# Heads in pairs on TensorE: scores from the two halves of the rows, values into the two halves of a bank

## The chip, the cores and the metric

The kernel runs on one core of one Trainium2 chip, as one program of 24,835 profiled instructions. The metric is the device time of one execution in microseconds, median of several runs. Engines are named as in the profile: PE is TensorE, PEld its weight loads, DVE is VectorE, ACT is ScalarE, POOL is GpSimd, SP is SyncE.

## What is computed

Two transformer blocks over 256 tokens of width 1024, in float32. The first has a gated spatial mixer, six heads of forgetting attention (fox: scores with a decay) and four heads that attend to 256 memory tokens, then a feed-forward layer. The second has two layers; each is a gated feed-forward layer, an attention, and another feed-forward layer. Its first attention is a sliding window with 16 heads over two key and value heads, its second a latent attention with 16 heads, whose queries and keys are 64 + 32 wide.

```python
# forgetting attention                       # memory attention
s = q @ k.T * scale + c_t - c_s              s = q @ km.T * scale
p = softmax(where(causal, s, NEG))           p = softmax(s)
o = p @ v                                    o = p @ vm
# sliding window                             # latent attention
scores = q @ k.T * scale + bias              s = q @ k.T * scale      # q, k 96 wide
p = softmax over window, with a sink         p = softmax(where(causal, s, NEG))
o = p @ v                                    o = p @ v
x = x + o.reshape(tokens, heads * 64) @ w_out
```

A head is 64 wide in the first three kinds.

## The kernel before

Nearly all the time goes into products of weights and activations. Weights come from HBM in chunks; `Stream` (`ws`) splits each into a high part (ScalarE, L102) and a low part (VectorE, L112), and every product is made of three passes in a reduced float32 format: high by high, high by low, low by high (`mm_t` L139 to L141, `mm_n` L149 to L151). The program is in order on each engine as it is written; the tile framework puts in the waits. PSUM has eight banks, handed out one tile a bank by `bank()`.

The attention of the heads is in plain float32, and one matmul of it stands in the trace as two records. It is made by `Pipe`, a pipeline by hand over heads ("units"), whose `step` is called between pieces of the weight products, so that TensorE has other work while VectorE and ScalarE do the softmax. Step n does, in this order:

- `score` of unit n (only at the start) and of unit n + 1: `attn_s`, two matmuls of the queries of 128 tokens each against the keys (L297), into a bank of its own. Queries and keys of a head 64 wide lie on rows 0 to 63 (even head) or 64 to 127 (odd head) of their tiles, so that these matmuls use 64 rows of TensorE; those of latent attention use 96. Fox heads then call `pre_fox` (L684, L685), which makes the decay products in another bank.
- `attn_t` of unit n - 2: three or four transpositions of the probabilities on TensorE (L308), and a copy to SBUF by ScalarE (`pt`, L311).
- on VectorE: the front of unit n (bias or mask, maximum: L695 to L705, L712 to L714, L979 to L987, L1215 to L1220), and `attn_tail` of unit n - 1 (reciprocal L286, scaling of the probabilities L289), mixed; then, if one is waiting, the low part of a finished output pair (`ol`, L331).
- `attn_exp` of unit n: exponentials on ScalarE (L271, L275).
- `attn_o` of unit n - 3: values, two matmuls with the 64 columns of the values as weights (L323, and L325 or L327). Even heads write rows 0 to 63 of a bank, odd heads rows 64 to 127 of the same bank; after the odd one ScalarE copies the bank out (`oh`, L330), and the low part is made in the next step (L331).
- `ws.low()`: the low part of the last weight chunk, where one waits (L112).

The pipeline runs three times: in the first block (units 0 to 5 are fox heads, 6 to 9 memory heads; steps among products of the mixer, then the gating matmuls L796), in the sliding window (16 units; two steps for each of the last six query products, with the norm products L995 and VectorE's L997 ahead of the first of them, and the rest in `out_proj_start`), and in latent attention (16 units; transpositions of the heads' keys and queries, L1228 and L1230, between the steps). Memory heads have 256 keys for both token halves (`w=(T, T)`), the others 128 for the first half and 256 for the second (`w=(P, T)`).

Of the kernel before, what the change touches and what calls it, by code (L numbers as in the profile page):

```python
# [9 lines left out]
F32 = mybir.dt.float32  # L10
# [4 lines left out]
ALU = mybir.AluOpType  # L15
AX = mybir.AxisListType

P = 128
T = 256
# [18 lines left out]
R_FORGET, R_SINK, R_QG, R_KG, R_FREQ, N_ROWS = 0, 6, 22, 54, 86, 102  # L38
# [12 lines left out]
def block_kernel(ctx: ExitStack, tc: tile.TileContext, a: dict, out: bass.AP, upto: int = 99):  # L51
# [11 lines left out]
    act, dve, gp, pe = nc.scalar, nc.vector, nc.gpsimd, nc.tensor  # L63

    def bank():
        return psp.tile([P, 512], F32, tag="ps", name="ps")
# [105 lines left out]
    rows = cst.tile([P, N_ROWS], F32, name="rows")  # L172
# [117 lines left out]

        return ops + [scaled(0, slice(0, w0)), scaled(1, slice(w0, w0 + w1))]

    def attn_s(u):
        w0, w1 = u["w"]
        ps = bank()
        for i, (o, n) in enumerate(((0, w0), (w0, w1))):
            pe.matmul(ps[:, o:o + n], lhsT=u["q"][:, i * P:i * P + P], rhs=u["k"][:, :n], start=True, stop=True)  # L297
        u["ps"] = ps
        if "pre" in u:
            u["pre"](u)  # L300

    def attn_t(u):
        w0, w1 = u["w"]
        pr = u["p"]
        pt = bank()
        blocks = [0, P, 2 * P] if w0 == P else [0, 2 * P, P, 3 * P]
        for j, b in enumerate(blocks):
            pe.transpose(pt[:, j * P:j * P + P], pr[:, b:b + P], ident)  # L308
        st = u["pp"].tile([P, w0 + w1], F32, tag="pt", bufs=2, name="pt")
        n = P * len(blocks)  # L310
        act.copy(st[:, :n], pt[:, :n])  # L311
        u["pt"] = st

    opair = {}

    def attn_o(u, oh, ol):
        i = u["o"]
        if i % 2 == 0:
            opair[0] = bank()
        ps = opair[0]  # L320
        r = ps[64 * (i % 2):64 * (i % 2) + 64]
        st, v = u["pt"], u["v"]
        pe.matmul(r[:, 0:T], lhsT=v[0], rhs=st[:, 0:T], start=True, stop=False)  # L323
        if u["w"][0] == P:
            pe.matmul(r[:, P:T], lhsT=v[1], rhs=st[:, T:T + P], start=False, stop=True)  # L325
        else:
            pe.matmul(r[:, 0:T], lhsT=v[1], rhs=st[:, T:2 * T], start=False, stop=True)  # L327
        if i % 2:
            k = i // 2
            act.copy(oh[k], ps[:, :T])  # L330
            opair[1] = lambda: dve.tensor_tensor(out=ol[k], in0=ps[:, :T], in1=oh[k].bitcast(F32), op=ALU.subtract)  # L331

    class Pipe:

# [11 lines left out]
            return self.units[i] if 0 <= i < len(self.units) else None  # L346

        def score(self, i):
            u = self.at(i)
            if u and "ps" not in u:  # L350
                attn_s(u)

        def step(self):
            i = self.n
            new, tail, tr, val = self.at(i), self.at(i - 1), self.at(i - 2), self.at(i - 3)
            self.score(i)
            self.score(i + 1)
            if tr:
                attn_t(tr)
            front = new["front"](new, new["ps"]) if new else []  # L360
            back = attn_tail(tail) if tail else []
            for op in front[:2] + back[:1] + front[2:4] + back[1:2] + front[4:] + back[2:]:
                op()
            if 1 in opair:
                opair.pop(1)()
            if new:
                attn_exp(new)
            if val:
                attn_o(val, self.oh, self.ol)
            ws.low()  # L370
            self.n += 1
            if self.done() and 1 in opair:
                opair.pop(1)()
# [177 lines left out]
    for nm, i0, i1 in seq:  # L551
        for i in range(i0, i1):
            src = [a[nm][i, 0], a[nm][i, 1]] if len(a[nm].shape) == 4 else [a[nm][i]]
            for ap in src:
                n = ap.shape[-1]
# [25 lines left out]
    with ExitStack() as es:  # L581
        mp = es.enter_context(tc.tile_pool(name="mix", bufs=1))
        pp = es.enter_context(tc.tile_pool(name="mixp", bufs=3))
# [8 lines left out]
        oh = [mp.tile([P, T], F32R, name=f"oh{k}") for k in range(KT)]  # L592
        ol = [mp.tile([P, T], F32R, name=f"ol{k}") for k in range(KT)]
# [15 lines left out]
        w = ws.get(0)  # L609
# [7 lines left out]
        for c in range(4):  # L617
            for tt in range(2):
                mm_n(pf[tt][:, :390], w, 0, 390, X, tt, [(2 * c, 0), (2 * c + 1, 1)], c == 0, c == 3)
            w = ws.get(min(4, c + 2))  # L620
# [65 lines left out]

        def front_fox(u, ps):
            h, pb = u["i"], u["pb"]
            s = pp.tile([P, 512], F32, tag="s", bufs=2, name="s")
            mx = sm.tile([P, 2], F32, tag="mx", bufs=3, name="mx")  # L690
            nm = sm.tile([P, 2], F32, tag="nm", bufs=3, name="nm")
            u["s"], u["nm"] = s, nm

            def decayed(i, o, n):
                return lambda: dve.scalar_tensor_tensor(  # L695
                    out=s[:, o:o + n], in0=pb[:, :n], scalar=ct[:, 6 * i + h:6 * i + h + 1],
                    in1=cmask[:, o:o + n], op0=ALU.add, op1=ALU.add)

            def scored(i, o, n):
                return lambda: dve.tensor_tensor_reduce(  # L700
                    out=s[:, o:o + n], in0=ps[:, o:o + n], in1=s[:, o:o + n], scale=1.0,
                    scalar=-3e38, op0=ALU.add, op1=ALU.max, accum_out=mx[:, i:i + 1])

            return [decayed(0, 0, P), decayed(1, P, T), scored(0, 0, P), scored(1, P, T),
                    lambda: dve.tensor_scalar(out=nm, in0=mx, scalar1=-1.0, scalar2=None, op0=ALU.mult)]  # L705
# [15 lines left out]
        for h in range(4):  # L721
            r = slice(64 * (h % 2), 64 * (h % 2) + 64)
            pipe.add(dict(q=mq[h // 2][r], k=km[h // 2][r], v=[vm[0][:, 64 * h:64 * h + 64], vm[1][:, 64 * h:64 * h + 64]],
                          w=(T, T), front=front_mem, o=12 + h))


        for i in range(2):
# [39 lines left out]
        for i in range(3):  # L767
            src = pu[i // 2][:, (i % 2) * T:(i % 2) * T + T]
            tile_x(src)
            if i == 0:  # L770
                vsq = []
                for tt in range(2):
                    act.activation(out=gv[tt], in_=pg[tt][:, :384], func=AF.Gelu_apprx_tanh, scale=rs_x[:, tt:tt + 1])
                    vsq.append(pp.tile([P, 512], F32, tag="s", bufs=2, name="vsq")[:, :384])
                    act.activation(out=vsq[tt], in_=gv[tt], func=AF.Square)
            pipe.step()
            if i == 0:
                for tt in range(2):
                    dve.tensor_reduce(out=vs[:, tt], in_=vsq[tt].rearrange("p (g d) -> p g d", g=6), axis=AX.X, op=ALU.add)
                dve.tensor_scalar(out=vs, in0=vs, scalar1=1.0 / 64, scalar2=EPS, op0=ALU.mult, op1=ALU.add)  # L780
                vr = sm.tile([P, 2, 6], F32, tag="vr", name="vr")
                rstd_pow(vr.rearrange("p a b -> p (a b)"), vs.rearrange("p a b -> p (a b)"), 12)
                for tt in range(2):
                    g3 = gv[tt].rearrange("p (g d) -> p g d", g=6)
                    gp.tensor_tensor(out=g3, in0=g3, in1=vr[:, tt, :, None].to_broadcast([P, 6, 64]), op=ALU.mult)
        for i in range(3):
            src = pu[i // 2][:, (i % 2) * T:(i % 2) * T + T]
            t = pp.tile([P, 512], F32, tag="s", bufs=2, name="ut")[:, :T]
            dve.tensor_tensor(out=t, in0=src, in1=rb, op=ALU.mult)
            act.activation(out=uT[i], in_=t, func=AF.Gelu_apprx_tanh)  # L790
        for j in range(3):
# [108 lines left out]
    with ExitStack() as es:  # L900
# [101 lines left out]
        for i in range(KT):  # L1002
            w = ws.get()
            p = bank()
            mm_t(p[:, :T], w, 0, P, X, range(4), True, False)
            if i == 1:
                pt = bank()
                for h in range(2):
                    for tt in range(2):
                        pe.transpose(pt[:, (2 * h + tt) * P:(2 * h + tt) * P + P], kn[tt][:, h].rearrange("p a d -> p (a d)"), ident)  # L1010
                for h in range(2):
                    act.copy(kT[h], pt[:, h * T:h * T + T])
            if i > 0:
                q_norm(i - 1)
            if i > 1:
                pipe.step()
            mm_t(p[:, :T], w, 0, P, X, range(4, KT), False, True)
            act.activation(out=qT[i], in_=p[:, :T], func=AF.Copy, scale=ga)
            qsq[i] = tp.tile([P, T], F32, tag="sq", name="sq")
            act.activation(out=qsq[i], in_=p[:, :T], func=AF.Square)  # L1020
            for h in (2 * i, 2 * i + 1):
                r = slice(64 * (h % 2), 64 * (h % 2) + 64)
                g = h // 8
                pipe.add(dict(q=qT[i][r], k=kT[g][r], v=[va[0][:, 64 * g:64 * g + 64], va[1][:, 64 * g:64 * g + 64]],
                              w=(P, T), front=front_swa, o=h, sink=rows[:, R_SINK + h:R_SINK + h + 1]))
            if i > 1:
                pipe.step()
        q_norm(KT - 1)
# [432 lines left out]
```

## Time and profile before

| | us |
|---|---|
| median of 3 runs | 1280.71 (1280.48 to 1282.17) |
| profiled execution | 1278.97 |
| its span, first to last instruction | 1277.1 |
| TensorE busy | 1250.2 (98%) |
| VectorE busy | 846.4 (66%) |
| ScalarE busy | 661.3 (52%) |
| mean granted clock of TensorE | 0.989 of full speed |

The busy time of TensorE counts its records from start to modelled end, and these overlap: a matmul's row tells when it starts, and the distance to the next start tells what it costs. "idle before" stands in brackets at the end of a timeline row, with the instruction that ended the wait.

### The profile page before, as it was taken

The page shows a single profiled execution, that of the slowest core. Times are in us where ns is not written, and L with a number is a line of the kernel's source. Part 1 is how long each engine was busy: PE and PEld are TensorE (multiplying, and loading weights), DVE is VectorE, ACT ScalarE, POOL GpSimd, SP SyncE. Part 2 cuts the span into 40 slices and gives each one's busy share as a digit, 9 for nine tenths or more (in the row PEclk, how much of TensorE's full clock was granted, in tenths as well). Part 3 has the DMA queues.
Part 4 walks back from the last instruction along what each step waited for, and adds up shares of the span by engine and source line. Part 5 has one row for each costly group of instructions (what it writes and reads, how often), then busy time and mean ns, then how long its engine had stood idle before and what let it go on. Part 6 is the DMA issues. An engine that isn't in the chain of part 4 may idle for free.

```text
span 1277.1 us, 24835 instructions
## 1 busy us (share of the span) xinstructions
PE 1250.2 (98%) x10316; PEld 1202.9 (94%) x10316; DVE 846.4 (66%) x1490; ACT 661.3 (52%) x1174; POOL 197.3 (15%) x192
## 2 busy tenths in 40 slices
PE   8999899999899999999999999999999989999998
PEld 7879899999799999977999999999999868999998
DVE  6886676654587666676766666666666796666553
ACT  5557465444345444565654444545454787554442
POOL 4424210110420001210300001100001462100000
PEclk9999899999899999999999999999999999999999
DMA  7534355555135545530455546556556411555463
GB/s 233 194 105 160 104 195 196 200 208 188 67 132 199 199 139 192 208 123 34 165 198 199 177 157 205 191 178 217 168 163 204 165 66 67 181 186 195 157 199 107
DMA packets 37265, 211.37 MB, mean 166 GB/s; under 512 B 4768, under 2 KB 8224, under 8 KB 18848
## 3 DMA queue, kind: packets, MB, share of 16 engines
q1 hardware_dynamic: 37152, 209.78, 48.3%
q8 instruction: 81, 1.33, 0.4%
q14 instruction: 32, 0.26, 0.1%
HBM read 208.71 MB, written 1.05 MB: 164 GB/s over the span
## 4 chain that ended last, share of the span: by engine, by line
PE 88%; DVE 6%; issue 2%; ACT 2%; DMA 1%; POOL 0%; SPq 0%; ACTq 0%; POOLq 0%; DVEq 0%
PE ps L139 26%; PE ps L140 26%; PE ps L141 26%; DVE wl L112 2%; PE ps L297 2%; PE ps L323 2%; PE ps L308 1%; PE ps L149 1%; PE ps L150 1%; PE ps L151 1%; PE ps L325 1%; ACT wh L102 1%; DVE dg L234 0%; PE ps L219 0%; DVE kc L1169 0%
## 5 line engine op out<-in xcount | busy, mean ns | idle before, releaser
L139 PE MATMUL ps<-xh,wh 128*128 128x256 f32 (+1 forms) x1848 | 523.0, 283 | 1.6 <-ACT xh L531 1.6
L140 PE MATMUL ps<-xl,wh 128*128 128x256 f32 (+1 forms) x1848 | 520.3, 282 | 1.5 <-DVE xl L538 0.8
L141 PE MATMUL ps<-xh,wl 128*128 128x256 f32 (+1 forms) x1848 | 518.9, 281 | 2.4 <-DVE wl L112 2.4
L112 DVE TENSOR_TENSOR wl<-raw,wh 128x1024 fp32r<-128x1024 f32 (+3 forms) x434 | 489.2, 1166 | 46.4 <-ACT wh L102 45.4
L102 ACT CAST wh<-raw 128x1024 fp32r<-128x1024 f32 (+4 forms) x436 | 400.2, 959 | 62.5 <-PE ps L140 26.5
L139 PEld LDWEIGHTS ps<-xh,wh 128*128 128x128 f32 (+1 forms) x1848 | 350.3, 190 | 5.3 <-issue 3.2
L140 PEld LDWEIGHTS ps<-xl,wh 128*128 128x128 f32 (+1 forms) x1848 | 349.8, 189 | 3.4 <-DVE xl L538 2.0
L141 PEld LDWEIGHTS ps<-xh,wl 128*128 128x128 f32 (+1 forms) x1848 | 350.0, 189 | 2.7 <-DVE wl L112 2.6
L139 PE MATMUL ps<-ah,wh 128*128 128x256 f32 x960 | 267.8, 279 | 0.0
L140 PE MATMUL ps<-al,wh 128*128 128x256 f32 x960 | 267.8, 279 | 0.0
L141 PE MATMUL ps<-ah,wl 128*128 128x256 f32 x960 | 267.8, 279 | 0.0
L139 PEld LDWEIGHTS ps<-ah,wh 128*128 128x128 f32 x960 | 180.4, 188 | 0.0
L140 PEld LDWEIGHTS ps<-al,wh 128*128 128x128 f32 x960 | 180.4, 188 | 0.0
L141 PEld LDWEIGHTS ps<-ah,wl 128*128 128x128 f32 x960 | 180.4, 188 | 0.0
L199 POOL TENSOR_TENSOR acc<-acc,sq 128x256 f32<-128x256 f32 x42 | 49.9, 1188 | 587.0 <-ACT sq L198 586.9
L393 ACT ACTIVATE s<-t 128x256 f32<-128x256 f32 x88 | 36.8, 418 | 191.9 <-DVE t L391 191.9
L391 DVE TENSOR_TENSOR t<-ps,rb 128x256 f32<-128x256 f32 x88 | 37.2, 423 | 73.5 <-PE ps L141 68.2
L213 DVE TENSOR_TENSOR al<-f,ah 128x256 fp32r<-128x256 f32 (+1 forms) x105 | 48.9, 466 | 52.8 <-ACT ah L212 52.8
L212 ACT CAST ah<-f 128x256 fp32r<-128x256 f32 (+1 forms) x105 | 45.9, 437 | 55.8 <-DVE f L395 43.2
L252 ACT ACTIVATE xh<-x,cols 128x256 fp32r<-128x256 f32 x40 | 20.4, 510 | 102.6 <-DVE x L428 95.6
L395 DVE TENSOR_TENSOR f<-ps,s 128x256 f32<-128x256 f32 x88 | 37.3, 424 | 47.4 <-ACT s L393 47.4
L427 DVE SCALAR_TENSOR_TENSOR t<-ps,rb 128x256 f32<-128x256 f32 x32 | 13.6, 425 | 76.2 <-PE ps L141 76.2
(285 smaller groups left out, 1321.4 us busy)
## 6 DMA issues: line engine op xcount, KB each, us to landing
raw<-in_gu SPq DMA_DIRECT2D x88, 1024.0 KB, 4.9
raw<-in_dn SPq DMA_DIRECT2D x64, 704.0 KB, 4.3
raw<-in_ff SPq DMA_DIRECT2D x32, 1024.0 KB, 5.0
raw<-in_w_out SPq DMA_DIRECT2D x4, 1024.0 KB, 4.9
raw<-in_aq SPq DMA_DIRECT2D x4, 1024.0 KB, 5.1
raw<-in_a_out SPq DMA_DIRECT2D x4, 1024.0 KB, 5.0
raw<-in_b_out SPq DMA_DIRECT2D x4, 1024.0 KB, 4.8
raw<-in_w1q SPq DMA_DIRECT2D x6, 512.0 KB, 4.0
```

Of the source, the lines that this page charges most:

```text
L102: act.copy(h[:, :n], t)
L112: eng.tensor_tensor(out=lo, in0=t, in1=h.bitcast(F32), op=ALU.subtract)
L139: pe.matmul(ps, lhsT=h[:, c:c + m], rhs=x[0][k], start=s0, stop=False)
L140: pe.matmul(ps, lhsT=h[:, c:c + m], rhs=x[1][k], start=False, stop=False)
L141: pe.matmul(ps, lhsT=lo[:, c:c + m], rhs=x[0][k], start=False, stop=s1)
L199: gp.tensor_tensor(out=acc, in0=acc, in1=sq, op=ALU.add)
L212: act.copy(h, src)
L213: dve.tensor_tensor(out=lo, in0=src, in1=h.bitcast(F32), op=ALU.subtract)
L297: pe.matmul(ps[:, o:o + n], lhsT=u["q"][:, i * P:i * P + P], rhs=u["k"][:, :n], start=True, stop=True)
L391: dve.tensor_tensor(out=t, in0=g, in1=rb, op=ALU.mult)
L393: act.activation(out=s, in_=t, func=AF.Silu)
L395: dve.tensor_tensor(out=f, in0=u, in1=s, op=ALU.mult)
```

## The change

Heads are taken in pairs in two places. `attn_s` takes one unit or two; with two, it takes two banks and issues the matmuls in turns: first tokens of the first head, first tokens of the second, then the other tokens of each. `score` makes a pair where the unit's number is even and both units are marked `halves`, as memory and sliding-window heads are; fox and latent heads are scored singly as before. So units n + 1 and n + 2 are scored in odd steps, and in even steps none. `attn_o` now always takes two units, the even one and the odd one, in the even step in which only the odd one was done before; it issues their first matmuls in turns, then their second ones. The transposed probabilities `pt` get three buffers instead of two, and the tile `s` of the first block is 384 columns wide instead of 512.

```diff
-    def attn_s(u):
-        w0, w1 = u["w"]
-        ps = bank()
+    def attn_s(*us):
+        for u in us:
+            u["ps"] = bank()
+        w0, w1 = us[0]["w"]
         for i, (o, n) in enumerate(((0, w0), (w0, w1))):
-            pe.matmul(ps[:, o:o + n], lhsT=u["q"][:, i * P:i * P + P], rhs=u["k"][:, :n], start=True, stop=True)
-        u["ps"] = ps
-        if "pre" in u:
-            u["pre"](u)
+            for u in us:
+                pe.matmul(u["ps"][:, o:o + n], lhsT=u["q"][:, i * P:i * P + P], rhs=u["k"][:, :n], start=True, stop=True)
+        for u in us:
+            if "pre" in u:
+                u["pre"](u)
...
-        st = u["pp"].tile([P, w0 + w1], F32, tag="pt", bufs=2, name="pt")
+        st = u["pp"].tile([P, w0 + w1], F32, tag="pt", bufs=3, name="pt")
...
-    def attn_o(u, oh, ol):
-        i = u["o"]
-        if i % 2 == 0:
-            opair[0] = bank()
-        ps = opair[0]
-        r = ps[64 * (i % 2):64 * (i % 2) + 64]
-        st, v = u["pt"], u["v"]
-        pe.matmul(r[:, 0:T], lhsT=v[0], rhs=st[:, 0:T], start=True, stop=False)
-        if u["w"][0] == P:
-            pe.matmul(r[:, P:T], lhsT=v[1], rhs=st[:, T:T + P], start=False, stop=True)
-        else:
-            pe.matmul(r[:, 0:T], lhsT=v[1], rhs=st[:, T:2 * T], start=False, stop=True)
-        if i % 2:
-            k = i // 2
-            act.copy(oh[k], ps[:, :T])
-            opair[1] = lambda: dve.tensor_tensor(out=ol[k], in0=ps[:, :T], in1=oh[k].bitcast(F32), op=ALU.subtract)
+    def attn_o(us, oh, ol):
+        ps = bank()
+        for part in range(2):
+            for i, u in enumerate(us):
+                r = ps[64 * i:64 * i + 64]
+                st, v = u["pt"], u["v"]
+                if part == 0:
+                    o, b = r[:, 0:T], st[:, 0:T]
+                elif u["w"][0] == P:
+                    o, b = r[:, P:T], st[:, T:T + P]
+                else:
+                    o, b = r[:, 0:T], st[:, T:2 * T]
+                pe.matmul(o, lhsT=v[part], rhs=b, start=part == 0, stop=part == 1)
+        k = us[0]["o"] // 2
+        act.copy(oh[k], ps[:, :T])
+        opair[1] = lambda: dve.tensor_tensor(out=ol[k], in0=ps[:, :T], in1=oh[k].bitcast(F32), op=ALU.subtract)
...
         def score(self, i):
-            u = self.at(i)
+            u, v = self.at(i), self.at(i + 1)
             if u and "ps" not in u:
-                attn_s(u)
+                pair = v and i % 2 == 0 and u.get("halves") and v.get("halves")
+                attn_s(u, v) if pair else attn_s(u)
...
-            if val:
-                attn_o(val, self.oh, self.ol)
+            if val and val["i"] % 2:
+                attn_o((self.at(i - 4), val), self.oh, self.ol)
...
-            s = pp.tile([P, 512], F32, tag="s", bufs=2, name="s")
+            s = pp.tile([P, 384], F32, tag="s", bufs=2, name="s")
...
-                          w=(T, T), front=front_mem, o=12 + h))
+                          w=(T, T), front=front_mem, o=12 + h, halves=True))
...
-                              w=(P, T), front=front_swa, o=h, sink=rows[:, R_SINK + h:R_SINK + h + 1]))
+                              w=(P, T), front=front_swa, o=h, halves=True, sink=rows[:, R_SINK + h:R_SINK + h + 1]))
```

## Rows read from the trace of the kernel before

**Rows 1.** The page, part 1: busy us, share of the span, instructions.

```profile
PE 1250.2 (98%) x10316; PEld 1202.9 (94%) x10316; DVE 846.4 (66%) x1490; ACT 661.3 (52%) x1174; POOL 197.3 (15%) x192
```

**Rows 2.** Busy time by stretch: start:end, length, then engines; clock, DMA share, GB/s.

```profile
543.00:606.00 63.00, 63.00 (x412) 48.81 (x412) 43.96 (x166) 38.30 (x124) 7.56 (x8) 1.00 0.21 78
43.00:108.00 65.00, 64.55 (x414) 52.64 (x413) 54.25 (x138) 33.39 (x80) 20.10 (x15) 0.97 0.40 132
1017.00:1073.00 56.00, 52.63 (x329) 41.37 (x328) 42.63 (x171) 42.89 (x123) 24.36 (x29) 0.97 0.17 57
```

**Rows 3.** Timeline of TensorE (start, length, line, tiles, count): a step with scores.

```profile
566.46 0.28 PE L141 MATMUL ps<-xh,wl 128*128 128x256 f32 x1
566.67 0.92 PE L297 MATMUL ps<-akT,aq 64*128 64x128 f32 x4
567.52 0.55 PE L308 MATMUL ps<-kon,p 128*128 128x128 f32 x3
```

**Rows 4.** Timeline of TensorE: a late step of the sliding window, without scores.

```profile
597.42 0.28 PE L141 MATMUL ps<-oh,wl 128*128 128x256 f32 x1
597.54 0.49 PE L308 MATMUL ps<-kon,p 128*128 128x128 f32 x3
597.96 0.65 PE L323 MATMUL ps<-pt,av 128*64 128x256 f32 x2
...
598.75 0.39 PE L139 MATMUL ps<-oh,wh 128*128 128x256 f32 x1
598.98 0.28 PE L140 MATMUL ps<-ol,wh 128*128 128x256 f32 x1
```

**Rows 5.** Timeline of TensorE: records of 128 columns in latent attention.

```profile
1030.73 0.38 PE L1228 MATMUL ps<-kon,kc 128*96 128x128 f32 x2
1030.95 0.38 PE L1230 MATMUL ps<-kon,qn 128*96 128x128 f32 x2
```

**Rows 6.** Timeline of TensorE: step 0 of the sliding window, heads 0 and 1.

```profile
543.11 0.93 PE L297 MATMUL ps<-akT,aq 64*128 64x128 f32 x8
```

**Rows 7.** Timeline of TensorE: the gating matmuls of the first block.

```profile
106.97 1.58 PE L796 MATMUL ps<-wst,gv 128*64 128x128 f32 x22
```

**Rows 8.** Timeline of TensorE: scores of a memory head.

```profile
73.89 1.13 PE L297 MATMUL ps<-km,mq 64*128 64x256 f32 x4
74.95 0.55 PE L308 MATMUL ps<-kon,p 128*128 128x128 f32 x3
```

**Rows 9.** Sliding window: busy time of two steps (columns as rows 2); VectorE's waits.

```profile
571.59:575.32 3.73, 3.73 (x25) 2.77 (x24) 3.73 (x15) 2.55 (x9) 0.51 (x1) 1.00 0.00 0
575.32:579.38 4.06, 4.06 (x28) 3.22 (x27) 1.80 (x10) 2.49 (x8) 0.50 (x1) 1.00 0.00 0
...
DVE rq L997 <- PE ps L995: 9.4, 6, 2.3
DVE den L285 <- ACT es L275: 4.3, 4, 1.4
```

**Rows 10.** First block: busy time of a stretch; timelines of VectorE and TensorE.

```profile
69.84:97.86 28.02, 28.02 (x161) 21.88 (x160) 26.50 (x60) 16.98 (x42) 9.42 (x5) 1.00 0.39 131
...
69.84 0.74 DVE L695 SCALAR_TENSOR_TENSOR s<-ps,ct,kmask 128x128 f32<-128x128 f32 x2 [2.03 <-PE ps L685]
90.41 2.29 DVE L289 TENSOR_SCALAR p<-p,rd 128x256 f32<-128x256 f32 x2
...
92.58 0.72 PE L308 MATMUL ps<-kon,p 128*128 128x128 f32 x4
```

**Rows 11.** Latent attention: busy time of a stretch; VectorE's first instruction in it.

```profile
1033.70:1058.00 24.30, 23.78 (x147) 17.15 (x147) 22.23 (x101) 21.32 (x69) 11.47 (x18) 1.00 0.12 44
...
1033.72 0.42 DVE L1233 COPY kT<-ps 96x256 f32<-96x256 f32 x1 [1.04 <-PE ps L1230]
```

**Rows 12.** Latent attention, start: a wait of TensorE; busy time of the stretch around it.

```profile
1026.42 0.87 PE L308 MATMUL ps<-kon,p 128*128 128x128 f32 x3 [2.76 <-DVE p L289]
...
1023.00:1030.00 7.00, 4.24 (x19) 3.80 (x19) 7.00 (x27) 4.97 (x14) 4.10 (x3) 0.76 0.41 146
```

More of the change, by code (lines that the diff above doesn't have):

```diff
@@ L773, in block_kernel @@
                     act.activation(out=gv[tt], in_=pg[tt][:, :384], func=AF.Gelu_apprx_tanh, scale=rs_x[:, tt:tt + 1])
-                    vsq.append(pp.tile([P, 512], F32, tag="s", bufs=2, name="vsq")[:, :384])
+                    vsq.append(pp.tile([P, 384], F32, tag="s", bufs=2, name="vsq"))
                     act.activation(out=vsq[tt], in_=gv[tt], func=AF.Square)
@@ L787, in block_kernel @@
             src = pu[i // 2][:, (i % 2) * T:(i % 2) * T + T]
-            t = pp.tile([P, 512], F32, tag="s", bufs=2, name="ut")[:, :T]
+            t = pp.tile([P, 384], F32, tag="s", bufs=2, name="ut")[:, :T]
             dve.tensor_tensor(out=t, in0=src, in1=rb, op=ALU.mult)
```

## The prediction

> **What bounds the kernel now.** I read the page's busy shares first: TensorE is busy 98% of a span of 1277.1 us [rows 1]. The change touches three attention stages alone, so next come their stretches (first block 43 to 108 us, sliding window 543 to 606, latent attention 1017 to 1073): TensorE is busy through nearly all of each, VectorE 54 of 65 us, 44 of 63 and 43 of 56 [rows 2]. So TensorE sets the end there, but VectorE stands close behind. Outside these stages the instructions stay the same, and I expect no difference there.
>
> Then I looked at what one head costs on TensorE, by when the next kind of matmul starts (lengths overlap and tell less). In a step of the sliding window with scores, the last weight matmul starts at 566.46 and the transpositions at 567.52 [rows 3]; in a late step without scores the same pair starts at 597.42 and 597.54 [rows 4]. The difference, 1.06 - 0.12 = 0.94 us, is the price of one head's scores. A float32 matmul stands as two records, and a record of 128 columns takes 0.11 us (two in 0.22) [rows 5], one of 256 twice that: the four records are 0.65 us of work. The other 0.3 us is the change from 128 rows to 64 and back. Values: the transpositions from 597.54 need 3 x 0.11, to 597.87; weight matmuls go on at 598.75, and their second starts 0.23 later where 0.12 is usual [rows 4]. So one head's values cost 0.88 + 0.11 = 0.99 us, of which 0.65 is work and 0.34 the change to 64 columns and back.
>
> **What pairing does to one pair.** The trace of before shows pairs twice. At the start of the sliding window, step 0 scores heads 0 and 1 one after the other: eight records take 0.93 us [rows 6], and four took 0.92 [rows 3]. One head lies on rows 0 to 63, the other on 64 to 127, and they run at the same time. For halves of columns there are the gating matmuls, which write the two halves of one bank: 22 records of 128 columns start and end within 1.58 us, where 22 x 0.11 would be 2.4 [rows 7]; the first of them are delayed by values ahead, so the bulk runs two at a time. So the second head of a pair costs nothing, neither its work nor its two changes of shape: a pair of values saves 0.99, a pair of scores 0.94. Memory heads have two 256-wide products: 73.89 to 74.95 is 1.06 us where the sliding window has 0.85 [rows 3, 8], so 0.21 more, for scores and values.
>
> Here a rule of the Trainium skill speaks against the change: "TensorE: Matmul & The Clock Gate", Part 3, on what overlaps, says that matmuls start and end strictly in program order. By that rule the listing order would limit the overlap (the third rival). The trace disagrees: before lists all of head 0's records ahead of head 1's, and still eight took 0.93 us [rows 6].
>
> **Count.** Sliding window: 8 pairs of values x 0.99 = 7.9; 7 of scores x 0.94 = 6.6 (the first pair is paired already): 14.5. First block: 3 fox pairs of values x 0.99 = 3.0, 2 memory pairs x 1.20 = 2.4, 2 pairs of memory scores x 1.15 = 2.3: 7.7. Latent attention: its scores use 96 rows and stay single; 8 pairs of values: 7.9. In all 30.1 us of TensorE time is taken away. What TensorE gets of it depends on who is late next.
>
> **Sliding window.** Two steps take 3.73 + 4.06 = 7.79 us, in which VectorE works 3.73 + 1.80 = 5.53 [rows 9]. TensorE's two steps become 7.79 - 0.99 - 0.94 = 5.9. VectorE's idle time is mostly a wait for TensorE's norm products (9.4 us in 6 waits), and that goes as TensorE comes sooner; 5.53 fits under 5.9. ScalarE's exponentials are the other guard: VectorE waited 4.3 us for them [rows 9]; each comes behind a copy of transposed probabilities, so it moves up with TensorE too. If none of it moved, 14.5 - 4.3 = 10.2 would be left; at best 14.5. I take 13.0, near the upper end, because most of the margin is a wait for TensorE: 1.5 off for the first heads, whose probabilities don't come sooner, and for the last.
>
> **First block.** VectorE is busy 26.5 of the 28.02 us from 69.84 to 97.86 [rows 10], so five of the seven savings fall where VectorE sets the pace: its scaling for one memory head runs from 90.41 to 92.70, while TensorE transposes that head from 92.58 [rows 10]. Before that stretch VectorE waits 2.03 us for TensorE's decay products [rows 10]; the first value block dropped, ahead of it, brings these forward by 1.0. Behind 92.6 two memory value blocks go, 2 x 1.2. That is 3.4; I take 3.0. Bounds: 1.0, if VectorE and ScalarE hold the tail as well, and 7.7. Queued behind a transposition that waits for VectorE are values and weight matmuls, all on TensorE, in order.
>
> **Latent attention.** From 1033.7 to 1058 VectorE is busy 22.23 of 24.30 us [rows 11]: of the five value blocks that go in it, only 2.1 us can be gained. One goes ahead of it, and VectorE's wait of 1.04 us for TensorE at its start [rows 11] says that this one counts in full; two go behind it, where VectorE is light. 1.0 + 2.1 + 2.0 = 5.1; I take 4.5. Bounds 2.0 (the last two alone) and 7.9.
>
> **Costs.** The edits add no instruction; a third buffer of transposed probabilities lets values wait a step, and the shorter score buffer pays for it in SBUF. The odd head's values stand where they stood, so copies and later products aren't moved. The paired scores hold two banks for up to two steps. If a transposition had to wait until VectorE's front of its own step has read one, that would cost up to a light step of VectorE, 1.80 [rows 9], in each of 10 pairs, 18 us; at the lower end nothing. I take nothing: counting tiles in program order, at most 8 of 8 banks are in use in the first block and 6 in the sliding window.
>
> **Sum.** 13.0 + 3.0 + 4.5 = 20.5 us. The profiled execution took 1278.97 us (1.9 more than its span) and becomes 1258.5; the median of the runs, 1280.71, stands 1.7 above it, so I forecast 1280.7 - 20.5 = 1260.2.
>
> **Rivals.**
> 1. VectorE and ScalarE hold harder: the low ends, 10.2 + 1.0 + 2.0 = 13.2, give 1267.5. For it: their busy shares; against: VectorE's long waits are for TensorE.
> 2. Nothing is given back: all 30.1, 1250.6. Against it: transpositions that start just as VectorE ends [rows 10].
> 3. Order counts: matmuls start as listed, each product's two records behind each other. Then a pair of scores runs 0.11 + 0.11 + 0.22 + 0.22 + 0.22 = 0.87 instead of 0.65, values the same, and each saving is about 0.22 less: 15 x 0.22 = 3.3 less in the sliding window, elsewhere hidden by VectorE. 17.2, 1263.5. The paired scores at the start of the sliding window speak against it [rows 6].
> 4. It doesn't do what it says for values: two sums being accumulated in one bank don't overlap. Only the changes of shape go, 0.34 a pair; sliding window 2.7 + 6.6 - 1.5 = 7.8, elsewhere about 3.5: 11.3, 1269.4. The gating products share a bank but accumulate nothing, so they don't exclude it.
> 5. Slower: TensorE's clock. Where TensorE waited 2.76 us for probabilities, the stretch around it shows a granted clock of 0.76, a part at 1.2 GHz [rows 12]. If waits on VectorE in latent attention now kept it at 1.2 GHz, its some 40 us less 8 saved, 32, would become 64: 24 more than now instead of 4.5 less, and with 16 gained elsewhere 1280.7 + 8 = 1289. [...]
>
> **How the numbers follow.** Forecast 0.55, rivals 0.20, 0.08, 0.08, 0.05, 0.04. The range 1254.0 to 1269.5 takes in the forecast's middle bounds and rivals 1, 3 and 4, and leaves out 2 and 5. About 0.2% is what a measurement can tell from no change. Faster 0.94, same 0.02 (rival 1 with banks running out), slower 0.04.
>
> **What would show it.** Eight score records in about 0.9 us in all odd steps of the sliding window; eight value records in about 1.0 us in even steps, none in odd; sliding window about 13 us shorter with VectorE over 85% busy; the first block and latent attention only some 3 and 4.5 us shorter, with TensorE idle ahead of transpositions, released by VectorE's scaling; all else the same length. A saving over 7 us in latent attention would say that VectorE didn't bind; a value block of 1.6 us, that halves of a bank don't overlap; waits of transpositions on VectorE's front, that banks run out.

## The result and the profile after

| | before | after |
|---|---|---|
| median of four runs each, us | 1280.60 (1277.5 to 1282.17) | 1259.85 (1257.58 to 1263.1) |
| ratio | 1 | 0.9853, 95% interval 0.9837 to 0.9869 |
| profiled execution, us | 1278.97 | 1259.43 |
| its span, us | 1277.1 | 1257.6 |

The forecast was 1260.2. In the changed kernel the lines stand a little lower: scores are L300, transpositions L311, values L332, the output copy and its low part L334 and L335, the gating matmuls L801. First the page's busy times, which answer to [rows 1], and the three stages, which answer to [rows 2] (sliding window, first block, latent attention; columns as there).

```profile
PE 1222.9 (97%) x10316; PEld 1187.9 (94%) x10316; DVE 846.2 (67%) x1490; ACT 660.1 (52%) x1174; POOL 196.1 (16%) x192
```

```profile
543.00:588.00 45.00, 43.85 (x367) 36.84 (x367) 41.78 (x160) 36.09 (x120) 6.04 (x6) 1.00 0.25 84
...
43.00:107.00 64.00, 57.80 (x414) 49.28 (x414) 55.79 (x142) 35.22 (x84) 19.95 (x15) 0.97 0.41 135
1001.50:1053.40 51.90, 46.51 (x332) 38.33 (x331) 43.42 (x172) 42.32 (x123) 24.36 (x29) 0.97 0.18 62
```

The counts of instructions are those of before, and VectorE, ScalarE and GpSimd are as busy as they were. Only TensorE lost busy time, 27.3 us, of which the span got 19.5. In the sliding window TensorE is still the full engine, with VectorE at 93%; in the first block it now stands idle for 6.2 of 64 us.

Where the 19.5 us lie can be read without any model, because both kernels issue the same 9312 weight matmuls in the same order: the start of each in the one trace less its start in the other.

| weight matmul | before, us | after, us | shift, us |
|---|---|---|---|
| first | 6.14 | 5.83 | -0.3 |
| within the first block's gating loop | 85.48 | 81.28 | -4.2 |
| first of the first block's output product | 108.47 | 107.34 | -1.1 |
| first of the sliding window, behind step 0 | 543.97 | 541.41 | -2.56 |
| behind the sliding window | 602.81 | 587.76 | -15.05 |
| first of the last output product | 1057.85 | 1040.34 | -17.5 |
| last | 1273.03 | 1253.46 | -19.57 |

So: first block 0.8 (forecast 3.0), sliding window 12.5 (13.0), latent attention 4.5 (4.5), and 1.4 between 108 and 340 us, where nothing was changed, with 0.3 before the first block.

### The profile page after: what moved, and what is told of

Read it like the earlier page. It is cut to its first block, busy times and chain, and to the rows that moved or that the text cites. A ratio compares the mean times of both kernels' runs of the same rounds, so it can differ in the third digit from the quotient of the medians.

```text
span 1257.6 us, 24874 instructions
## 1 busy us (share of the span) xinstructions
PE 1222.9 (97%) x10316; PEld 1187.9 (94%) x10316; DVE 846.2 (67%) x1490; ACT 660.1 (52%) x1174; POOL 196.1 (16%) x192
## 4 chain that ended last, share of the span: by engine, by line
PE 83%; DVE 9%; issue 3%; ACT 2%; DMA 1%; POOL 1%; SPq 0%; ACTq 0%; POOLq 0%; DVEq 0%
PE ps L139 26%; PE ps L140 26%; PE ps L141 25%; DVE wl L112 3%; PE ps L300 1%; PE ps L311 1%; PE ps L332 1%; DMA raw<-in_w1q 1%; PE ps L149 1%; PE ps L150 1%; ACT wh L102 1%; PE ps L151 1%; DVE p L289 1%; ACT p L271 0%; DVE dg L234 0%
## 5 line engine op out<-in xcount | busy, mean ns | idle before, releaser
L432 DVE SCALAR_TENSOR_TENSOR t<-ps,rb 128x256 f32<-128x256 f32 x32 | 13.6, 425 | 76.9 <-PE ps L141 76.9
```

## Experiments

My theory was that of the forecast: two heads on the two halves of TensorE run at the same time; what comes of it is decided stage by stage by the engine that is next, VectorE above all. The rivals were the forecast's third (the listing order counts) and fourth (only the changes of shape are saved), that the two halves of the change help each other, and, in the first block and latent attention, that a chain of latencies holds and not VectorE's amount of work. Every ratio below is to the kernel before, run beside the kernel in question.

### Values in pairs alone, scores in pairs alone

In the changed kernel, once the scores as before and once the values as before (the old `attn_o`, one head a step); the first is one line:

```diff
-                pair = v and i % 2 == 0 and u.get("halves") and v.get("halves")
+                pair = False
```

> The changed kernel with values in pairs and every head's scores single, as before. Theory (each stage is held by its own engine): the sliding window gains 8 x 0.95 = 7.6 us, latent attention the 4.5 it gained with the whole change, the first block the 1.1 that VectorE lets through: 13.2 us under the kernel before, ratio 0.9897, some 1267.4. Rival (VectorE already holds the sliding window after the whole change, so the two parts overlap): values alone give nearly all there is, 11 of the window's 12.7, and the ratio is under 0.987.

> The changed kernel with scores in pairs and every head's values single, as before. Theory: 7 pairs x 0.96 = 6.7 us in the sliding window, nothing in latent attention (it has no score pairs), nothing in the first block (its two pairs lie where VectorE sets the pace): ratio 0.9948, some 1274. Rival (parts overlap): 9 to 11 us of the window, ratio 0.992.

Values alone took 1268.04 us, ratio 0.991 (0.9891 to 0.993); scores alone 1273.59, ratio 0.9955 (0.9939 to 0.9971). Both agree with the theory's 0.9897 and 0.9948. In the sliding window, by the shifts of the weight matmuls, each pair of values brought 0.98 us and each pair of scores 0.93 to 1.0, but the first one 0.5; scores alone brought 0.3 us in latent attention, where they are single. The savings below 1, 0.0090 and 0.0045, add up to 0.0135, and the whole change has 0.0147: two additive parts, within the intervals. The window's shifts are finer: 7.4 us for values and 6.2 for scores make 13.6, and the whole change brought 12.5 there (12.7 in the first expectation, which counts from 340 us on), since the second pair of scores also brought only 0.5 and a wait behind the stage, below, grew. The rival of the first run, that values alone bring 11, fell.

### Scores from one half of the rows

```diff
-                pipe.add(dict(q=qT[i][r], k=kT[g][r], ...
+                pipe.add(dict(q=qT[i][:64], k=kT[g][:64], ...
```

(and the same for memory heads)

> The changed kernel with both heads of a pair scored on rows 0 to 63: it leaves out the odd heads' own queries and keys and takes the even head's a second time. The order of instructions is the same, and the two heads of a pair now share a half of the rows. Theory (the two halves of the rows work at the same time): each pair's scores take four more records behind each other, 0.65 us, in 8 pairs of the sliding window 5 us (2 pairs of memory scores are hidden behind VectorE): 1265, ratio 0.989. Rival (the gain of paired scores is only that TensorE changes between 128 and 64 rows half as often): no change to the changed kernel, 1260, ratio 0.985.

1264.15 us, ratio 0.9891 (0.9873 to 0.991): the theory's number. By the shifts the sliding window gained 8.3 us instead of 12.5, so 4.2 less, where 5 were expected. The timelines of TensorE, first of the changed kernel, then of this one, show the pair itself (start, length, line, tiles, count):

```profile
563.19 0.53 PE L311 MATMUL ps<-kon,p 128*128 128x128 f32 x3
563.64 0.87 PE L332 MATMUL ps<-pt,av 128*64 128x256 f32 x8
564.44 0.39 PE L139 MATMUL ps<-xh,wh 128*128 128x256 f32 x1
...
566.06 0.93 PE L300 MATMUL ps<-akT,aq 64*128 64x128 f32 x8
566.91 0.55 PE L311 MATMUL ps<-kon,p 128*128 128x128 f32 x3
```

```profile
561.80 1.57 PE L300 MATMUL ps<-akT,aq 64*128 64x128 f32 x8
563.31 0.55 PE L311 MATMUL ps<-kon,p 128*128 128x128 f32 x3
```

Eight records on two halves take 0.93 us, eight on one half 1.57: the overlap is worth 0.64. The other 0.3 of a pair's 0.95 is still saved by pairs on one half (0.94 in the step without scores, less 0.66 for the longer pair); I take it for the change of shape that falls away. The values tell the same: eight records from 563.64, weights again 0.80 later, where before four records held TensorE for 0.79 [rows 4].

### One head after the other

```diff
-        for part in range(2):
-            for i, u in enumerate(us):
+        for i, u in enumerate(us):
+            for part in range(2):
```

(in `attn_s` likewise)

> The changed kernel with all matmuls of the first head of a pair listed ahead of all of the second's, for scores and values. Theory (the halves of TensorE run their matmuls side by side however they are listed, as heads 0 and 1 did in the kernel before): no change against the changed kernel, within 0.1%, some 1260, ratio 0.985; a pair's eight score records still start within 0.6 us. Rival (matmuls start in the order listed): a pair takes about 1.1 us of work instead of 0.65, 15 x 0.45 = 6.7 us lost in the sliding window, some 1267, ratio 0.990.

1259.73 us, ratio 0.9856 (0.9835 to 0.9877): no difference. With all matmuls of the first head listed ahead of the second's, TensorE's timeline shows the same two lengths:

```profile
565.22 0.93 PE L300 MATMUL ps<-akT,aq 64*128 64x128 f32 x8
...
568.69 0.88 PE L332 MATMUL ps<-pt,av 128*64 128x256 f32 x8
```

The turns that the change writes out are not what pays; that the two heads stand next to each other is. By the rule of the Trainium skill ("TensorE: Matmul & The Clock Gate", Part 3), that matmuls start and end in program order, this kernel would have lost most of the overlap; the measurement decides against it for this case.

### The masks' work moved out of the gating loop

In the first block VectorE and GpSimd also make masks for the second block, in the gating loop (GpSimd's subtraction L513, VectorE's comparison L515). Moved behind the gating as one piece, then spread over the output product, then the latter in the kernel before:

```diff
-            t5_mask(c, [n5[:, c % 2]], [o5[:, c]])
...
+        rel_parts()
+        for c in range(4):
+            t5_mask(c, [n5[:, c % 2]], [o5[:, c]])
```

> The changed kernel with the preparation for the sliding window's bias (the bias parts on VectorE, four masks on GpSimd and VectorE) moved from the first block's attention to behind its gating matmuls. Theory (VectorE, and behind it GpSimd's scaling of the gates, held the first block): with some 9 us of VectorE's work and 9 us of GpSimd's out of the stage, TensorE keeps most of the 7.7 us that it lost there: 3 to 5 us more than the changed kernel, some 1256, ratio 0.982, unless the moved work delays the output product. Rival (a chain of exponentials and copies held it): no change, ratio 0.985.

> The changed kernel with GpSimd's and VectorE's work for the masks of the second block taken out of the gating loop of the first block: the relative positions come behind the gating, and the four masks are spread over the evictions of the output product, one subtraction on GpSimd and one comparison on VectorE for each, so that no long row of them stands ahead of VectorE's low parts of the weights. Theory (VectorE, slowed beside GpSimd, holds the first block, and the gating products hang on GpSimd's scaling): the first block becomes some 4 to 6 us shorter, as in late_t5 (4.1 us ahead by the gating products, although it had started 2.1 us late), and nothing is given back in the output product: about 1255 us, ratio 0.981. Rival (the same work delays the low parts wherever it stands): the output product gives it back, 1260 us or more, ratio 0.985 or over.

> The same move of the masks in the kernel before, with heads taken singly. Theory (unpaired, the first block is nearly all TensorE's, so that VectorE's relief is worth little): 0 to 2 us less than before, 1279 to 1281, ratio 0.998 to 1.0, so that pairing on top of the move (the run beside it) brings about 24 us where it brought 20.5. Rival (the relief is worth the same with or without pairs, because the gating products hang on GpSimd in both): 4 to 6 us less, 1275, ratio 0.996 or under.

As one piece 1268.75 us, ratio 0.9927 (0.9906 to 0.9948); spread 1264.37, ratio 0.9881 (0.9865 to 0.9897); spread in the kernel before 1287.31, ratio 1.0071 (1.0058 to 1.0084). All three are slower than the kernel they were made from; the first two were expected faster, the third at most 2 us faster. As an improvement the move failed, but its two halves can be read apart. The first block gained what the theory says: by the shift of the weight matmuls from 74 us to the output product's first, TensorE gained 6.1 us on the changed kernel in both (2.0 and 1.3 of it made up a late start, the rest put it 4.1 and 4.8 ahead), and only 0.3 us on the kernel before where heads are taken singly (that execution was 4.8 us late by 60 us, before the stage that the move touches, 4.5 at the output product and 12.8 behind the norm). So the masks held the block only once heads were paired, as far as one trace of each tells. The medians fit: pairing on top of the spread masks is worth 22.9 us, where 24 were expected and 20.8 were measured without the move. Then the output product gave back more. First the one-piece kernel, TensorE's waits from 100 to 140 us and VectorE's timeline; then the spread one, the timelines of TensorE and GpSimd (in brackets: idle time before, and what ended it):

```profile
PE ps L141 <- DVE wl L112: 9.5, 1, 9.5
...
119.42 3.50 DVE L515 TENSOR_SCALAR o<-n,cols 128x1024 bf16<-128x1024 int32 x2 [1.78 <-POOL n L513]
122.84 6.82 DVE L112 TENSOR_TENSOR wl<-raw,wh 128x1024 fp32r<-128x1024 f32 x5
```

```profile
131.60 0.58 PE L219 MATMUL ps<-kon,macc 128*128 128x1 f32 x2 [5.62 <-POOL macc L199]
...
125.88 1.70 POOL L199 TENSOR_TENSOR macc<-macc,sq 128x256 f32<-128x256 f32 x1
127.54 2.34 POOL L820 TENSOR_TENSOR n<-posr,posc 128x1024 int32<-128x1024 int32 x1
129.84 1.70 POOL L199 TENSOR_TENSOR macc<-macc,sq 128x256 f32<-128x256 f32 x1
```

In one piece the masks stood ahead of five low parts in VectorE's queue. Spread, they stood between GpSimd's sums of squares, and the norm's matmul waited 5.62 us for the last sum (5.8 in the kernel before with the same move).

### The low part of the outputs left out

```diff
-        opair[1] = lambda: dve.tensor_tensor(out=ol[k], in0=ps[:, :T], in1=oh[k].bitcast(F32), op=ALU.subtract)
```

> The changed kernel without the low part of the attention outputs of memory, sliding-window and latent heads: it leaves out VectorE's subtraction for each pair (18 of them, 0.4 to 0.5 us each), and the output products read the high part in its place, so that TensorE's work is the same. Theory (VectorE holds latent attention and part of the first block): about 2 us less in latent attention, 1 in the sliding window where a weight load of the output product waits 0.8 us for the low part, 0.7 in the first block: 1256.5, ratio 0.983. Rival (VectorE is idle often enough, and what holds is a chain of latencies from TensorE to VectorE and back): 1 us or less, 1259 to 1260, ratio 0.985.

1260.44 us, ratio 0.9846 (0.9833 to 0.9858): the rival's number. By the shifts against the changed kernel, the 0.8 us wait in the sliding window went, the first block gained some 0.3 of the 0.7 expected and latent attention nothing; 2.1 us were lost between 108 and 500 us, where both kernels do the same, so the whole time alone decides little. For the start of latent attention the shifts don't settle it either. The chain of work that ended last (start, length, work), in this kernel and then, one pair later, in the changed one:

```profile
1025.43 0.89 PE ps L311 x3
1026.32 1.48 PE ps L332 x8
```

```profile
1029.43 0.61 PE ps L311 x3
1030.04 0.80 PE ps L332 x8
```

The stretch of TensorE at 1.2 GHz fell here on a pair's transpositions and values (0.7 us more on the values alone), in the changed kernel on weight matmuls around 1013 us; against that stand five subtractions left out, 2.1 us of VectorE. The middle of the stage is clearer. From the transposition at 1029.43 to the first weight matmul of the output product at 1040.34, both at full clock, every matmul of this kernel starts 0.94 to 0.96 us behind the changed kernel's, so the pace is the same. Yet VectorE has less to do, as ten of those microseconds show, in this kernel and then in the changed one (columns as [rows 2]):

```profile
1031.00:1041.00 10.00, 9.74 (x76) 7.66 (x77) 8.52 (x46) 9.99 (x34) 1.64 (x1) 1.00 0.00 1
```

```profile
1031.00:1041.00 10.00, 9.73 (x76) 7.93 (x75) 9.38 (x50) 9.99 (x34) 1.64 (x1) 1.00 0.00 1
```

VectorE is busy 8.52 us instead of 9.38, so its amount of work doesn't hold that part. ScalarE may, since it has no gap in either kernel (9.99 of 10.00 us). No run here changes ScalarE's work, so that stays open.

### The first block's chain: gating weights masked early, gating values shared

```diff
         rbm = bcast(rs_m, "rbm")
+        gp.tensor_tensor(out=wst, in0=wst, in1=uone[:, None, :P].to_broadcast([P, 6, P]), op=ALU.mult)
...
-                gp.tensor_tensor(out=wst, in0=wst, in1=uone[:, None, :P].to_broadcast([P, 6, P]), op=ALU.mult)
```

```diff
-                for tt in range(2):
-                    g3 = gv[tt].rearrange("p (g d) -> p g d", g=6)
-                    gp.tensor_tensor(out=g3, in0=g3, in1=vr[:, tt, :, None].to_broadcast([P, 6, 64]), op=ALU.mult)
+            if i < 2:
+                g3 = gv[i].rearrange("p (g d) -> p g d", g=6)
+                (gp, dve)[i].tensor_tensor(out=g3, in0=g3, in1=vr[:, i, :, None].to_broadcast([P, 6, 64]), op=ALU.mult)
```

> The changed kernel with one GpSimd instruction moved: the masking of the gating weights (1.80 us, at 89.34 us, beside which VectorE's scaling of a memory head took 2.23 us where 0.6 is usual) comes ahead of the masks' work, right behind the norm of the memory, where GpSimd is otherwise idle from 53.6 to 72.9 us. Theory (VectorE, slowed beside GpSimd, holds the transpositions of the memory heads, and what follows hangs on them): the wait of 2.46 us ahead of the transpositions at 91.44 falls to about 0.9, and the gating products come 1.6 us sooner: 1258.2, ratio 0.984. Rival (the chain behind, from ScalarE's table load to the gating, does not hang on these transpositions): the wait falls, but the gating products start where they did, 1259.8, ratio 0.9853.

> The changed kernel with the scaling of the gating values shared: the first 128 tokens stay on GpSimd (1.32 us), the other 128 go to VectorE (about 0.55) one step later. Theory (the gating products, and with them the rest of the kernel, wait for a chain of VectorE's sums, GpSimd's power and GpSimd's two scalings): the waits of 1.41 and 0.36 us ahead of the gating products shrink by 1.3 in all: 1258.5, ratio 0.9843. Rival (the output product's low parts on VectorE, or GpSimd's later products, take the place of that wait): no change to the changed kernel, 1259.8, ratio 0.9853; above that, if VectorE's wait for GpSimd's power holds up a low part that TensorE needs.

> Both moves in one kernel: the masking of the gating weights early, the scaling of the gating values shared by GpSimd and VectorE. Theory: both waits of the first block shrink, 1.6 + 1.3 = 2.9 us under the changed kernel: 1257, ratio 0.983. Rival (one of them only moves the wait to the other): the better one of the two alone, 0.984 or more.

In the first block the waits did what the theory says. TensorE's waits from 80 to 112 us (line and what it waited for: us in all, times, longest) of the early masking, and of both moves together:

```profile
PE ps L311 <- DVE p L289: 2.4, 2, 1.5
PE ps L801 <- POOL gv L790: 1.8, 2, 1.4
```

```profile
PE ps L311 <- DVE p L289: 2.4, 2, 1.5
PE ps L801 <- POOL gv L790: 0.8, 1, 0.8
```

The changed kernel has 4.0 and 1.8 there (next section). With the masking early, VectorE's scaling at 88.94 us took 0.60 us instead of 2.23. With the scalings shared and nothing else moved, no wait for GpSimd is left ahead of the gating; GpSimd ended its half at 103.4 us, 2.4 sooner than both halves in the changed kernel, and 1.0 of that is an earlier start of the chain. With both moves TensorE comes sooner and waits 0.8 us for GpSimd's half again. By the shift of the weight matmuls from 74 us on, the early masking came 1.65 us ahead by the last query product, both moves together 3.0 us ahead by the output product; expected were 1.6 and 2.9. The shared scalings alone came only 0.8 ahead by the output product, for 1.3, since a stretch at 1.2 GHz (granted clock 0.50 from 92 to 94 us, 1.00 in the changed kernel) had put TensorE 1.55 us back just before.

The whole times say less: 1260.72, 1259.71 and 1259.68 us, ratios 0.9842 (0.9827 to 0.9858), 0.9831 (0.9816 to 0.9845) and 0.9832 (0.9816 to 0.9849), against 0.9853 of the changed kernel. All are lower, none by more than the intervals; the early masking's profiled execution had lost 1.5 us of its gain again by the first matmuls of the output product, and the rest by 195 us, in steps of 0.5 us, where the kernels are the same. That both moves together beat the changed kernel is likely, by some 2 us, and not shown.

## Why the prediction was right, and where it was not

**The price of a pair, and that halves overlap: right.** Forecast 0.94 for scores and 0.99 for values; the shifts of the sliding window grow by 0.95 and 0.96 from step to step. The third and fourth rivals (1263.5 and 1269.4) fell with the listing order and with the values' eight records in 0.87 us.

**Sliding window: right, 12.5 for 13.0** (12.3 to 12.5 in the traces of six other kernels that leave the window as in the changed one). VectorE gave way as argued, because its idle time was waiting for TensorE. The waits of 540 to 592 us of the changed kernel, against 9.4 and 4.3 [rows 9]:

```profile
DVE rq L1002 <- PE ps L1000: 1.6, 4, 0.6
...
PEld ps L140 <- DVE ol L335: 1.0, 1, 1.0
DVE den L285 <- ACT es L275: 0.9, 3, 0.5
```

The middle line is new: behind the stage, the output product gave back 0.9 us, for a low part. The forecast had taken 1.5 off for the first and last heads. Measured are 2.0: the first two pairs of scores brought 0.51 and 0.53 instead of 0.94, with transpositions that wait 0.2 us each for VectorE's scaling (546.08 and 551.36 us), as foreseen; the rest is mostly that low part, which the forecast didn't name.

**Latent attention: the sum right, 4.5 for 4.5, its parts not all.** The last two value blocks brought 1.0 each, as forecast. The other six were to bring 1.0 for the first, in full, and 2.1 for five. Measured: the first head's transposition (1026.42 in before [rows 12], 1011.41 after) came 15.0 us sooner, the fifth's (1039.74 and 1024.55) 15.2, the first weight matmul of the output product 17.5. So the early blocks brought 0.2 and the middle ones 2.3. That VectorE's work leaves room for no more was the forecast's reason. For the middle, from 1029 us on, the run without the low parts speaks against it: with less work on VectorE the pace stayed. So the 2.3 there for 2.1 may be right for another reason, and what holds the early part stays open.

**First block: wrong, 0.8 for 3.0** (1.4 and 1.5 with one head after the other and with scores on one half, where the block's other work is the same). The step that failed is "Behind 92.6 two memory value blocks go, 2 x 1.2." Up to 92.6 us the forecast held: savings ran 4.2 us ahead, then TensorE waited for VectorE's scaling, and VectorE was 1.1 us sooner (89.32 instead of 90.41 [rows 10]) where 1.0 was forecast. The two later value blocks did bring TensorE forward again, to -3.5 at 99.62 us. But then the gating matmuls waited. The changed kernel's TensorE (waits from 80 to 110 us and timeline), and its VectorE and GpSimd:

```profile
PE ps L311 <- DVE p L289: 4.0, 2, 2.5
PE ps L801 <- POOL gv L790: 1.8, 2, 1.4
...
91.44 0.72 PE L311 MATMUL ps<-kon,p 128*128 128x128 f32 x4 [2.46 <-DVE p L289]
```

```profile
88.04 1.36 DVE L719 SCALAR_TENSOR_TENSOR nm<-mx,smem 128x2 f32<-128x2 f32 x1
89.32 2.23 DVE L289 TENSOR_SCALAR p<-p,rd 128x256 f32<-128x256 f32 x2
...
93.99 0.16 DVE L719 SCALAR_TENSOR_TENSOR nm<-mx,smem 128x2 f32<-128x2 f32 x1
94.13 0.62 DVE L289 TENSOR_SCALAR p<-p,rd 128x256 f32<-128x256 f32 x2
...
87.48 1.90 POOL L513 TENSOR_TENSOR n<-posr,posc 128x1024 int32<-128x1024 int32 x1 [2.75 <-DVE o L515]
89.34 1.80 POOL L769 TENSOR_TENSOR wst<-wst,kon 128x768 f32<-128x768 f32 x1
100.84 2.27 POOL L188 TENSOR_TENSOR vr<-vs,mhalf 128x12 f32<-128x12 f32 x1 [9.70 <-DVE vs L785]
103.18 2.64 POOL L790 TENSOR_TENSOR gv<-gv,vr 128x384 f32<-128x384 f32 x2
```

VectorE's sums (L785), GpSimd's power (2.27 us) and its two scalings (2.64) are a chain behind VectorE's stretch, and it moved only by VectorE's 1.1. It could have been seen before: there the same scalings run like this, to 106.92 us, and the gating matmuls start in bulk at 106.97 [rows 7].

```profile
104.27 2.65 POOL L785 TENSOR_TENSOR gv<-gv,vr 128x384 f32<-128x384 f32 x2
```

TensorE and GpSimd arrived together, so no saving of TensorE alone could pass that point. The forecast's lower end, 1.0, "if VectorE and ScalarE hold the tail as well", was the case, but by GpSimd, which the forecast had left out of the block. The run that shared the scalings took this wait away, the early masking 1.6 us of the other.

**All else the same length: off by 1.7 us, in the other direction.** Before the first block the changed kernel was 0.3 us ahead. Between 108 and 340 us the shift went from -1.1 back to -0.6 at 138.6, to -1.9 from 142.9 to 145.5 and to -2.5 by 340. In both kernels TensorE runs a part of these places at 1.2 GHz, as the granted clock shows (third column from the end); before, then after:

```profile
136.00:148.00 12.00, 10.43 (x76) 9.88 (x77) 8.07 (x20) 4.38 (x9) 5.31 (x7) 0.72 0.00 1
326.00:342.00 16.00, 13.11 (x80) 11.62 (x81) 13.54 (x27) 7.41 (x17) 8.71 (x10) 0.68 0.00 1
```

```profile
133.00:145.00 12.00, 9.16 (x68) 8.32 (x68) 9.95 (x20) 4.07 (x8) 7.18 (x7) 0.72 0.13 52
323.00:339.00 16.00, 12.70 (x81) 11.03 (x78) 14.28 (x27) 6.94 (x17) 9.85 (x10) 0.68 0.00 1
```

The mean clock is the same; how much work falls on the slow part and how much on waits isn't. In the kernel before, the weight matmuls from 142.71 to 143.77 us still start 0.21 us apart, in the changed one those from 142.07 on 0.12. This is no effect of pairing: from 108 to 500 us, where eight more of the kernels do the same work as the changed one, they lie between 2.4 us ahead of the kernel before and 0.7 behind it, and from 603 to 1000 us four of the traces drift back by 1.8 us and the others by none. So it was luck that this 1.7 made up for most of the terms that fell short, 2.2 in the first block and 0.5 in the sliding window. The two profiled executions differ by 19.5 us, the medians by 20.8, for 20.5: the total is better than its terms.

**The rivals on VectorE and on the clock.** That another engine would hold harder than forecast (1267.5) was true of one stage in three, and there it was GpSimd behind VectorE. The slower case didn't come: TensorE does wait in latent attention, but the stage's clock is 0.97 as before [rows 2]. Banks cost nothing, as taken: the only wait of a transposition for VectorE's front is one of 0.3 us, of a weight load in the sliding window.

## What to carry to other kernels

When an engine is relieved, look for the places in the old trace where another chain arrives at the same moment; a saving passes such a point only if both chains get it, and a wait of zero in front of it doesn't show there is room. Work for a later stage that was free while TensorE was full may set the pace afterwards, and moving it costs whatever stands behind it in its new queue. Effects of 1 to 3 us are safer read from the shift of the same instructions in two traces than from whole times, in stretches where both ran at the same clock.

## What was not expected of the hardware

**Small VectorE instructions beside GpSimd.** A product of 2 columns took 1.36 us at 88.04, while GpSimd's subtraction ran from 87.48 to 89.38, and 0.16 at 93.99 with GpSimd idle; the scaling of two halves 2.23 us beside GpSimd's masking of weights, 0.62 without. Moving the masking away brought the first of these scalings to 0.60. By the Trainium skill, "SBUF — State Buffer", section on the two separate sides, the two engines share a pair of ports that one instruction holds to its end. The trace agrees: the product of 2 columns ends at 89.40 us, GpSimd's subtraction at 89.38; so does the early masking, with 1.6 us gained.

**The order in which matmuls on two halves are listed** made no difference (0.9853 and 0.9856), with two sums accumulated in one bank as well (0.87 and 0.88 us for eight records).
